# FoX layer of a two-layer trunk: V split as v^T and transposed by DMA, a query pair's scores and output products each in one block, and the opening's order written by hand

## The chip, the cores and the metric

The kernel runs on one core of a Trainium2 chip. The metric is the device time of one launch in microseconds (us), taken as the median of three runs.

## What is computed

`reference(x, ...)` runs two layers and a final norm on x of 1024 tokens by 1024 features, float32:

```python
for i in range(2):
    h = rmsnorm(x, norm_g[i])
    x = x + (fox_mixer(h, ...) if i == 0 else nsa_mixer(h, ...))
return rmsnorm(x, final_g)

def fox_mixer(h, w_in, b_f, w_out):            # 16 heads of 64
    q, k, v, f, z = split(h @ w_in)
    c = cumsum(log_sigmoid(f + b_f))            # one number per token and head
    logits = q @ k.T / 8 + c[query] - c[key]    # causal
    return (softmax(logits) @ v * silu(z)) @ w_out
```

The change concerns layer 0 (`fox_mixer`) alone. Layer 1, a sparse attention with three branches, follows layer 0's output projection.

## The kernel before

**Projections.** `to_hT` transposes the normed x on TensorE (PE) into `hT`, two halves of 512 tokens, each as a high and a low part (`fp32r`). A projection of 128 columns is `project` (L135): per half 8 steps of three 128x512 matmuls (`mm3`, L131 to L133: high by high, high by low, low by high), 24 in all. The weights of one head pair and kind are loaded by `load_w` (into the single buffer `wst`), split on VectorE and GpSimd, and kept two ahead in the queue `wq` by `next_w`.

**Head pairs.** The 16 heads go as 8 pairs p. `fox_fill` is the list of projections: for each pair K, V, Q and Z, with the forget gate behind pair 0's K. It may run up to two pairs ahead of the attention; it waits for `("scored", p - 2)` before K's buffers are written again and for `("done", p - 2)` before V's are.

**V.** `fox_v` copies the projection v^T (128 columns of a pair x 512 tokens) from PSUM to `vT` (ScalarE, L385), transposes it in four 128x128 blocks on PE into the PSUM tile `ptv` (L363, `fox_v_transposes`, issued four steps into the next projection), and splits it into three bf16 parts of 64 columns that stand side by side for each head and key tile: ScalarE (L366, L368), VectorE (L367), GpSimd (L369). So the 192 columns of a head's V are one run in `v`.

**Attention.** A `FoxDuo` is two query tiles of one head: u = 0 is tile 4 + x (5 to 8 key tiles), u = 1 is tile 3 - x; together 9 key tiles. `score(u)` makes the scores in pieces of up to 512 keys (two matmuls each, L523 and L524, into one of three PSUM buffers of `psS`), adds the bias and takes the running minimum on VectorE (L532), then takes the exponential (ScalarE, L541), a float16 high part (ScalarE, L542) and the low part (VectorE, L543) into `hl`, and sends both to `pT` by a transposing DMA (L544, on SP's queue). `pv(u)` multiplies with V: for each key tile a product of the high part with all 192 columns (L555) and one of the low part with 128 (L556), so a pair of products per key tile and 9 pairs per duo. `finish` sums the three parts on VectorE (L570), scales into `o` (L572), and after a pair's last duo transposes `o` on PE (L579, `pto`), multiplies with silu(z) and stores to `oF`.

**What sets the order.** `fox_main` runs 64 duos; step n does score(0) of duo n, pv(0) of duo n - 2, score(1) of duo n, pv(1) of duo n - 2, then `finish` of duo n - 2. Every generator yields a booked cost, and `merge` (L190) interleaves: after each yield of `fox_main` it runs `fox_fill` until the fill's booked sum has reached `PACE` (2.25, or `LAST` = 1.6 for the last eight duos) times what `fox_main` has booked. Booked are 650 per projection step, 450 per group of transposes, 570 per four pairs of products. `pv` yields after every four key tiles, so projections can come between. Engines run their instructions in this order; SP's DMA queue too.

**The opening.** A loop over the eight tiles of x loads, norms and transposes, two tiles behind; the norm's multiplies of tiles 2 and 5 are on GpSimd, the others on VectorE (L104). At tile 3, `next_w(False)` loads the first two weights, so `wst_v` stands on SP's queue ahead of the last tile, x_7. Then come K of pair 0, the forget gate, V of pair 0.

**The end.** When pair 7's projections are done, `load_wout` loads and splits the output weights in `hT`'s place, `out_start` starts the first tile of the output projection, and `out_layer` does the rest. `out_start` waits only for its last piece on `("o", 7, 1)`.

Of the kernel before, what the change touches and what calls it, by code (L numbers as in the profile page):

```python
# [33 lines left out]
def f(ap):  # L34
    return ap.bitcast(F32)
# [3 lines left out]
def tile_fox_nsa(ctx, tc, a, out):  # L39
# [212 lines left out]
    fox_order = [x for p in range(8) for x in ((1, p), (2, p), (0, p), (3, p))]  # L252
# [7 lines left out]
    gB = st.tile([P, D], F32, name="gB")  # L260
    pend = []
    for t in range(NT):
        xt = st.tile([P, D], F32, tag="x", bufs=7, name=f"x_{t}")
        dma(xt, a["x"][t * P:(t + 1) * P, :])
        if t == 0:
            dma(gB, a["norm_g"][0:1, :].to_broadcast([P, D]))
        nm = Norm(st, xt, f"n0_{t}", 3)
        nm.square(slice(0, D))
# [6 lines left out]
    for x in pend:  # L275
        to_hT(*x)
    dma(tri, a["tri"])


    wfst = st.tile([P, KC, H], F32, name="wfst")  # L280
    dma(wfst, a["fox_w_f"].rearrange("(k p) c -> p k c", p=P))
    bf = st.tile([H, 1], F32, name="bf")
    dma(bf, a["fox_b_f"].rearrange("o h -> h o"))
    below = st.tile([P, P], F32, name="below")
    dma(below, a["below"])
    wf = st.tile([P, KC, P], F32R, name="wf")
    G.tensor_copy(wf, zero[:, :, None].to_broadcast([P, KC, P]))
    V.tensor_copy(wf[:, :, 0:H], wfst)
    V.tensor_tensor(wf[:, :, 32:32 + H], wfst, f(wf[:, :, 0:H]), OP.subtract)

    def forget_gate():
        fT = st.tile([H, S], F32, name="fT")
        f2 = st.tile([H, S], F32, name="f2")
        for half in range(2):
            pt = ps_a(f"pf_{half}")
            ts = slice(half * 512, half * 512 + 512)
            for k in range(KC):
                T.matmul(pt, wf[:, k, :], hT[half][0][:, k, :], start=(k == 0), stop=False)
# [25 lines left out]
        V.tensor_tensor(e3[:, 1:, :], e3[:, 1:, :], r[:, 0:3, None].to_broadcast([P, 3, 32]), OP.add)  # L324
        pt = ps_t("pc")
# [8 lines left out]
    def fox_k(p):  # L334
        KH = [sa.tile([P, S], F32R, tag="KH", bufs=4, name=f"KH_{p}_{j}") for j in range(2)]
        KL = [sa.tile([P, S], F32R, tag="KL", bufs=4, name=f"KL_{p}_{j}") for j in range(2)]
        w = next_w()
        for half in range(2):
            ts = slice(half * 512, half * 512 + 512)
            pt = ps_a(f"k{p}_{half}")  # L340
            yield from project(w, hT, half, pt)
            for j in range(2):
                r, o = rows[j], rows[1 - j]
                A.copy(KH[j][r, ts], pt[r, :])
                V.tensor_tensor(KL[j][r, ts], pt[r, :], f(KH[j][r, ts]), OP.subtract)
                dma(f(KH[j][o, ts]), f(KH[j][r, ts]))
                dma(f(KL[j][o, ts]), f(KL[j][r, ts]))
        ready["k", p] = KH, KL

# [9 lines left out]
    def fox_v_transposes(vt, half, vT, name):  # L359

        pv = ps_t(f"ptv_{name}")
        for i in range(4):
            T.transpose(pv[:, i * P:(i + 1) * P], vT[:, i * P:(i + 1) * P], ident)  # L363
        v4, r = (x.rearrange("p (t j d) -> p j t d", t=4, j=2) for x in (pv, vT))
        v1, v2, v3 = (vt[:, :, 4 * half:4 * half + 4, 64 * i:64 * i + 64] for i in range(3))
        A.copy(v1, v4)  # L366
        V.tensor_tensor(r, v4, v1, OP.subtract)  # L367
        A.copy(v2, r)  # L368
        G.tensor_tensor(v3, r, v2, OP.subtract)  # L369

    def fox_v(p):
        w = next_w()
        vt = sa.tile([P, 2, NT, 192], BF16, tag="v", bufs=2, name=f"v_{p}")
        pend = []
        for half in range(2):
            pt = ps_a(f"v{p}_{half}")
            n = 0
            for c in project(w, hT, half, pt):
                yield c
                n += 1  # L380
                if n == 4 and pend:
                    fox_v_transposes(*pend.pop())
                    yield 450
            vT = sb[0].tile([P, 512], F32, tag="P", bufs=7, name=f"vT_{p}_{half}")
            A.copy(vT, pt)  # L385
            pend.append((vt, half, vT, f"{p}_{half}"))
        ready["v", p] = vt
        ready["later"] = pend

    def fox_q(p, w, halves=(1, 0)):  # L390
        Q = ready.setdefault(("qt", p), {})
        for half in halves:
            pt = ps_a(f"q{p}_{half}")
            n = 0
            for c in project(w, hT, half, pt):
                yield c
                n += 1
                if n == 4 and ready["later"]:
                    fox_v_transposes(*ready["later"].pop())
                    yield 450  # L400
# [16 lines left out]
    def fox_fill():  # L417
        for p in range(8):
            if p >= 2:
                yield lambda p=p: ("scored", p - 2) in ready  # L420
            yield from fox_k(p)
            if p == 0:
                yield from forget_gate()
                sb.append(tc.alloc_tile_pool(name="sb", bufs=2, reuse_waits="tile"))
            if p >= 2:
                yield lambda p=p: ("done", p - 2) in ready
            yield from fox_v(p)
            wo_copy(0, p)
# [8 lines left out]
    def out_start():  # L437
# [3 lines left out]
        for c in (slice(0, 4), slice(4, 7), slice(7, 8)):  # L441
            if c.stop == KC:
                yield lambda: ("o", 7, 1) in ready
# [38 lines left out]
    class FoxDuo:  # L482
# [19 lines left out]
        def score(self, u):  # L502
            p, j = self.p, self.j
            if u == 0:
                yield from self.pre()
# [10 lines left out]
            for c in range(s + 1):  # L516
# [4 lines left out]
                Ls.append((L, n))  # L521
# [17 lines left out]
            for c, (L, n) in enumerate(Ls):  # L539
# [6 lines left out]
        def pv(self, u):  # L546
# [38 lines left out]

    def fox_main():
        duos = [FoxDuo(p, j, x) for p in range(8) for j in range(2) for x in range(4)]
        for n in range(len(duos) + 2):
            if n == len(duos) - 8:
                yield (LAST,)  # L590
            for u in range(2):
                if n < len(duos):
                    yield from duos[n].score(u)
                    if u and duos[n].j == 1 and duos[n].x == 3:
                        ready["scored", duos[n].p] = True
# [732 lines left out]
```

## Time and profile before

| what | value |
| --- | --- |
| median of 3 runs | 1609.14 us (1608.29 to 1612.16) |
| the profiled execution's own time | 1609.73 us |
| its span in the profile | 1607.7 us |
| PE (matmul) busy | 1527.3 us, 95% |
| VectorE (DVE) busy | 1132.1 us, 70% |
| ScalarE (ACT) busy | 870.4 us, 54% |
| GpSimd (POOL) busy | 545.1 us, 34% |
| DMA, mean | 130 GB/s |

Layer 0 takes up to the last `finish` at 610.4 us and the output projection behind it. The page's shares are means over both layers. A line's busy time counts an instruction from its start to its modelled end; since matmuls are pipelined, the next one starts earlier than that, and what a matmul costs is read from one start to the next.

### The profile page before, as it was taken

To read this page: it belongs to the slowest core of one execution; us is meant where nothing else is said; L and a number is where in the kernel's file an instruction comes from. 1 tells how busy PE (TensorE), PEld (TensorE's weight loads), DVE (VectorE), ACT (ScalarE), POOL (GpSimd) and SP (SyncE) were. 2 spreads that over 40 slices of the span, in tenths; PEclk is the share of its full clock that TensorE was granted. 3 is DMA by queue.
4 is the path that set the end of the run, shared out by engine and by line. 5 is a ranking of instruction groups with operands and counts; after the bars stand their busy time and mean duration, and the time that the engine had idled before them with its cause. 6 is when DMAs were issued, how large, how long until landed. Compare 5 with 4: busy or idle time off the path is not lost.

```text
span 1607.7 us, 26181 instructions
## 1 busy us (share of the span) xinstructions
PE 1527.3 (95%) x8600; PEld 1269.1 (79%) x8600; DVE 1132.1 (70%) x2867; ACT 870.4 (54%) x2126; POOL 545.1 (34%) x584
## 2 busy tenths in 40 slices
PE   6999999999999868999999989999999999999898
PEld 5887777777777656878888777788888888888786
DVE  6377777777777884355654686788888888888633
ACT  5255545555555662223232545578778778787522
POOL 3232223323223110032333223446646547554200
PEclk9999999999999979999999999999999999999999
DMA  7676666657657675441535645511312312212442
GB/s 241 226 143 134 128 160 131 153 113 149 156 114 160 151 153 165 133 155 60 162 104 154 218 151 193 204 54 63 122 53 66 119 40 79 73 40 93 147 148 92
DMA packets 237431, 209.11 MB, mean 130 GB/s; under 512 B 162737, under 2 KB 184497, under 8 KB 237041
## 3 DMA queue, kind: packets, MB, share of 16 engines
q1 hardware_dynamic: 237296, 207.46, 47.3%
q8 instruction: 68, 1.11, 0.3%
q14 instruction: 67, 0.54, 0.1%
HBM read 123.26 MB, written 46.20 MB: 105 GB/s over the span
## 4 chain that ended last, share of the span: by engine, by line
PE 60%; DVE 18%; ACT 9%; issue 7%; DMA 4%; POOL 1%; SPq 0%; DVEq 0%; POOLq 0%; ACTq 0%
PE ptp_n L1186 6%; PE S_n L1162 6%; DVE P L532 4%; PE y L131 3%; PE y L132 3%; PE y L133 3%; PE O_n L1195 3%; PE O_n L1194 3%; DVE hl L543 3%; ACT P L541 3%; DMA wo<-wD 1%; ACT cP L969 1%; PE nz L131 1%; ACT hl L542 1%; PE nz L132 1%
## 5 line engine op out<-in xcount | busy, mean ns | idle before, releaser
L1174 POOL TENSOR_SCALAR P_n<-P_n,l_n,gates 128x640 f32<-128x640 f32 (+7 forms) x256 | 200.9, 791 | 179.8 <-DVE l_n L1172 146.0
L541 ACT ACTIVATE P<-P,m 128x256 f32<-128x256 f32 (+1 forms) x192 | 117.0, 610 | 164.2 <-DVE m L532 163.8
L144 DVE TENSOR_TENSOR ptl_n<-ptp_n,pth_n 128x512 fp32r<-128x512 f32 (+1 forms) x272 | 181.4, 672 | 33.8 <-ACT pth_n L143 30.1
L1170 ACT ACTIVATE P_n<-P_n,m_n 128x640 f32<-128x640 f32 (+7 forms) x256 | 188.5, 737 | 24.9 <-DVE m_n L1169 22.8
L143 ACT CAST pth_n<-ptp_n 128x512 fp32r<-128x512 f32 (+1 forms) x272 | 153.8, 569 | 72.7 <-PE ptp_n L1186 71.5
L1186 PE MATMUL ptp_n<-ident,P_n 128*128 128x128 f32 x1056 | 167.1, 275 | 5.4 <-DVE ptl_n L144 3.6
L1162 PE MATMUL S_n<-nk,nq 128*128 128x320 f32 (+5 forms) x768 | 171.1, 333 | 0.2 <-DVE m_n L1169 0.2
L512 POOL TENSOR_TENSOR Bd<-B,tri 128x128 f32<-128x128 f32 x128 | 65.0, 509 | 302.3 <-DVE m L532 284.9
L1186 PEld LDWEIGHTS ptp_n<-ident,P_n 128*128 128x128 f32 x1056 | 124.4, 140 | 31.9 <-DVE ptl_n L144 9.3
L1194 PE MATMUL O_n<-pth_n,nv 128*128 128x512 f32 (+3 forms) x384 | 140.1, 369 | 1.0 <-DVE ot_n L1205 0.7
L543 DVE SCALAR_TENSOR_TENSOR hl<-P,hl 128x256 f16<-128x256 f32 (+1 forms) x192 | 126.4, 686 | 19.4 <-ACT hl L542 17.8
L1162 PEld LDWEIGHTS S_n<-nk,nq 128*128 128x128 f32 x768 | 128.0, 188 | 15.2 <-DVE m_n L1169 1.6
L1195 PE MATMUL O_n<-ptl_n,nv 128*128 128x512 f32 (+3 forms) x384 | 120.6, 338 | 0.1
L1169 DVE CUSTOM_DVE_ANT_0 P_n<-S_n,wmask 128x128 f32<-128x128 f32 (+1 forms) x192 | 113.3, 591 | 9.0 <-PE S_n L1162 4.1
L555 PE MATMUL O<-v,pT 128*128 128x192 bf16 x576 | 104.1, 255 | 12.3 <-DMA pT<-hl 10.8
L131 PE MATMUL y<-wo,oh 128*128 128x512 f32 x256 | 103.1, 403 | 9.0 <-ACT oh L627 4.0
L132 PE MATMUL y<-wo,oh 128*128 128x512 f32 x256 | 102.3, 400 | 0.0
L133 PE MATMUL y<-wo,ol 128*128 128x512 f32 x256 | 101.4, 397 | 0.0
L555 PEld LDWEIGHTS <-pT 128*128 128x128 f16 x576 | 57.4, 100 | 54.6 <-issue 40.4
L556 PE MATMUL O<-v,pT 128*128 128x128 bf16 x576 | 97.7, 224 | 0.0
L542 ACT ACTIVATE hl<-P 128x256 f16<-128x256 f32 (+1 forms) x192 | 92.5, 513 | 2.5 <-DMA pT<-hl 0.8
L1194 PEld LDWEIGHTS O_n<-pth_n,nv 128*128 128x128 f32 x384 | 72.6, 189 | 7.0 <-DVE ot_n L1205 1.3
(346 smaller groups left out, 4077.7 us busy)
## 6 DMA issues: line engine op xcount, KB each, us to landing
nq<-qD SPq DMA_DIRECT2D x64, 256.0 KB
B<-cD SPq DMA_DIRECT2D x16, 512.0 KB
wo<-wD SPq DMA_DIRECT2D x16, 512.0 KB
nq<-qD SPq DMA_DIRECT2D x64, 128.0 KB
of<-oF SPq DMA_DIRECT2D x14, 512.0 KB
x<-in_x_dram SPq DMA_DIRECT2D x8, 512.0 KB
wst_k<-in_fox_w_dram SPq DMA_DIRECT2D x8, 512.0 KB
wst_v<-in_fox_w_dram SPq DMA_DIRECT2D x8, 512.0 KB
```

What stands on the lines that cost most here:

```text
L131: T.matmul(ps, wh, mh, start=first, stop=False, **kw)
L132: T.matmul(ps, wh, ml, start=False, stop=False, **kw)
L144: V.tensor_tensor(lo[:, 0:n], pt[:, 0:n], f(hi[:, 0:n]), OP.subtract)
L541: A.activation(L[:, 0:n], L[:, 0:n], AF.Exp, bias=init, scale=-1.0, accum_out=self.lr[:, col + c:col + c + 1])
L543: V.scalar_tensor_tensor(lo[:, cs], L[:, 0:n], UP, hi[:, cs], OP.mult, OP.subtract)
L555: T.matmul(po[:, 0:192], self.hT[:, b0 + k, :], v[:, self.j, k, :], start=(k == 0), stop=False)
L1162: T.matmul(ps[:, b, 0:w], self.q[x][:, qi * P:(qi + 1) * P], k[:, k0 + b * w:k0 + b * w + w], start=(x == 0), stop=(x == 1))
L1170: A.activation(L, L, AF.Exp, bias=m, scale=-1.0, accum_out=lr[:, 0, qi:qi + 1])
L1174: G.tensor_scalar(L, L, lr[:, 1, qi:qi + 1], gates[:, i, x:x + 1], OP.mult, OP.mult)
L1186: T.transpose(pt[:, (x + i) * P:(x + i + 1) * P], L[:, kb * P - k0:(kb + 1) * P - k0], ident)
L1194: T.matmul(po[:, d], v, hi[:, c], start=(b == i == 0), stop=False)
L1195: T.matmul(po[:, d], v, lo[:, c], start=False, stop=(b == len(self.blocks) - 1 and i == len(pieces) - 1))
```

## The change

**V.** `fox_v` splits v^T itself, straight from PSUM, into three bf16 rows of 512 in `vs` (one buffer): ScalarE (L397, L399), VectorE (L398), GpSimd (L400). One transposing DMA per half (L401, 12 blocks of 128x128) puts them in `v`. There is no group of transposes on PE, no `vT` and no `ptv`. In `v` the three parts of a key tile now lie 512 elements apart, so that a product's right operand is three runs of 64.

**Blocks.** Step n of `fox_main` does the scores of both tiles of duo n (the short one first, and within a tile the last piece first), and then all nine pairs of products of duo n - 2 followed by `finish`; `burst` sums the booked costs and yields once, so that no projection comes between.

**Opening.** A function orders PE, VectorE and ScalarE by hand: all eight norms on VectorE, each tile transposed one step behind its norm, only K's weights loaded by it, x_7 before `wst_v` on SP's queue, and the forget gate's and K's steps mixed in from tile 5 on. K of pair 0 is a generator `k0`, the gate `gate0`.

**End.** `out_start` waits for each of its pieces by its own `("o", p, 1)`.

```diff
-    def fox_v_transposes(vt, half, vT, name):
...
     def fox_v(p):
         w = next_w()
-        vt = sa.tile([P, 2, NT, 192], BF16, tag="v", bufs=2, name=f"v_{p}")
...
+        v = sa.tile([P, 2, 3, 4, P], BF16, tag="v", bufs=2, name=f"v_{p}")
         for half in range(2):
             pt = ps_a(f"v{p}_{half}")
...
+            yield from project(w, hT, half, pt)
+            vs = sa.tile([P, 3, 512], BF16, tag="vs", bufs=1, name=f"vs_{p}_{half}")
...
+            A.copy(vs[:, 0], pt)
+            V.tensor_tensor(r, pt, vs[:, 0], OP.subtract)
+            A.copy(vs[:, 1], r)
+            G.tensor_tensor(vs[:, 2], r, vs[:, 1], OP.subtract)
+            nc.sync.dma_start_transpose(v[:, half].rearrange("p c t d -> p (c t) d"), vs.rearrange("p c t -> p (c t)"))
...
     def fox_q(p, w, halves=(1, 0)):
...
-                if n == 4 and ready["later"]:
-                    fox_v_transposes(*ready["later"].pop())
-                    yield 450
+            yield from project(w, hT, half, pt)
...
-            for c in range(s + 1):
+            for c in range(s, -1, -1):
...
+            po = po[:, 0:192].rearrange("p (c d) -> p c d", c=3)
             for k in range(nk):
-                T.matmul(po[:, 0:192], self.hT[:, b0 + k, :], v[:, self.j, k, :], start=(k == 0), stop=False)
-                T.matmul(po[:, 0:128], self.hT[:, b0 + nk + k, :], v[:, self.j, k, 0:128], start=False, stop=(k == nk - 1))
-                if k % 4 == 3:
-                    yield 570
-            if nk % 4:
-                yield 142 * (nk % 4)
+                vk = v[:, k // 4, :, k % 4, 64 * self.j:64 * self.j + 64]
+                T.matmul(po, self.hT[:, b0 + k, :], vk, start=(k == 0), stop=False)
+                T.matmul(po[:, 0:2], self.hT[:, b0 + nk + k, :], vk[:, 0:2], start=False, stop=(k == nk - 1))
+            yield 142 * nk
...
-            for u in range(2):
-                if n < len(duos):
-                    yield from duos[n].score(u)
...
-                if n >= 2:
-                    yield from duos[n - 2].pv(u)
+            if n < len(duos):
+                yield from burst(duos[n].score(u) for u in (1, 0))
...
             if n >= 2:
+                yield from burst(duos[n - 2].pv(u) for u in (0, 1))
                 yield from duos[n - 2].finish()
```

and of the opening:

```diff
-        h = nm.finish(gB, 1, G if t in (2, 5) else None)
-        pend.append((h, t, hT, f"n0_{t}", (ps_s, ps_t)))
-        if t >= 2:
-            to_hT(*pend.pop(0))
-        if t == 3:
-            next_w(False)
...
+        with tc.manual_schedule(engines={T.engine, V.engine, A.engine}):
+            for t in range(NT + 1):
+                if t < NT:
+                    nm = Norm(st, xs[t], f"n0_{t}", 3)
+                    nm.square(slice(0, D))
+                    hs[t] = nm.finish(gB)
+                if t:
+                    to_hT(hs.pop(t - 1), t - 1, hT, f"n0_{t - 1}", (ps_s, ps_t))
+                if t == 1:
+                    V.tensor_copy(whi, wst)
+                    G.tensor_tensor(wlo, wst, f(whi), OP.subtract)
...
+                if t == 4:
...
+                    side = [k0] * 9 + [gate0] * 8
+                if t >= 5:
+                    for g in side[0:5]:
+                        next(g)
...
```

In PE's order up to the output projection there are 174 blocks of output products before and 66 now; behind 144 and 52 of them stands a projection matmul. Layer 1's order is unchanged.

PE at the end of pair 1 (k3 is the K projection of pair 3, O_1_1_3 the products of the pair's last duo, pto its o transposes), before:

```order
L131 MATMUL k3_1_2326<-hT0_1_0_96,whi_k3_2046 128x512
L132 MATMUL k3_1_2326<-hT0_1_1_97,whi_k3_2046 128x512
L133 MATMUL k3_1_2326<-hT0_1_0_96,wlo_k3_2047 128x512
L555 LDWEIGHTS pT_1_1_3_2063
L555 MATMUL O_1_1_3_2280<-v_1_868,pT_1_1_3_2063 128x192
L556 LDWEIGHTS pT_1_1_3_2063
L556 MATMUL O_1_1_3_2280<-v_1_868,pT_1_1_3_2063 128x128
L131 MATMUL k3_1_2326<-hT0_1_0_96,whi_k3_2046 128x512
L132 MATMUL k3_1_2326<-hT0_1_1_97,whi_k3_2046 128x512
L133 MATMUL k3_1_2326<-hT0_1_0_96,wlo_k3_2047 128x512
L579 MATMUL pto_1_1_2344<-ident_72,o_1_1668 128x128 x3
```

And now, the last pair of products, then the projection matmuls up to the transposes (of twelve, six are left out):

```order
L567 LDWEIGHTS pT_1_1_3_2046
L567 MATMUL O_1_1_3_2282<-v_1_861,pT_1_1_3_2046 128x192
L568 LDWEIGHTS pT_1_1_3_2046
L568 MATMUL O_1_1_3_2282<-v_1_861,pT_1_1_3_2046 128x128
L131 MATMUL k3_1_2309<-hT0_1_0_96,whi_k3_2023 128x512
L132 MATMUL k3_1_2309<-hT0_1_1_97,whi_k3_2023 128x512
L133 MATMUL k3_1_2309<-hT0_1_0_96,wlo_k3_2024 128x512
...
L132 MATMUL k3_1_2309<-hT0_1_1_97,whi_k3_2023 128x512
L133 MATMUL k3_1_2309<-hT0_1_0_96,wlo_k3_2024 128x512
L588 MATMUL pto_1_1_2327<-ident_72,o_1_1656 128x128 x4
L131 MATMUL k3_1_2309<-hT0_1_0_96,whi_k3_2023 128x512
```

The products are no longer split by projections; between the last of them and the transposes stand twelve projection matmuls instead of three.

ScalarE at the V projection of pair 2 (P and hl rows are the exponentials and high parts of the scores), before:

```order
L385 COPY vT_2_0_1726<-v2_0_1646 128x512
L541 ACTIVATE P_1_0_3_1_0_1736,l_1_0_3_1676<-P_1_0_3_1_0_1736,m_1_0_3_1_1734 128x128
L542 ACTIVATE hl_1_0_3_1674<-P_1_0_3_1_0_1736 128x128
L366 CAST v_2_1645<-ptv_2_0_1777 128x2x4x64
L541 ACTIVATE P_1_1_0_0_0_1770,l_1_1_0_1765<-P_1_1_0_0_0_1770,m_1_1_0_0_1768 128x512
L368 CAST v_2_1645<-vT_2_0_1726 128x2x4x64
L542 ACTIVATE hl_1_1_0_1763<-P_1_1_0_0_0_1770 128x512
L541 ACTIVATE P_1_1_0_0_1_1787,l_1_1_0_1765<-P_1_1_0_0_1_1787,m_1_1_0_0_1768 128x128
L542 ACTIVATE hl_1_1_0_1763<-P_1_1_0_0_1_1787 128x128
L385 COPY vT_2_1_1834<-v2_1_1728 128x512
L541 ACTIVATE P_1_1_0_1_0_1829,l_1_1_0_1765<-P_1_1_0_1_0_1829,m_1_1_0_1_1827 128x512
```

And now (vs is the split's buffer, of which there is one; the row vs_2_1 is the first to write it for the second half):

```order
L397 CAST vs_2_0_1729<-v2_0_1643 128x512
L399 CAST vs_2_0_1729<-vr_2_0_1730 128x512
L551 ACTIVATE P_1_1_0_1_0_1766,l_1_1_0_1761<-P_1_1_0_1_0_1766,m_1_1_0_1_1764 128x512
L551 ACTIVATE P_1_1_0_0_1_1779,l_1_1_0_1761<-P_1_1_0_0_1_1779,m_1_1_0_0_1777 128x128
L552 ACTIVATE hl_1_1_0_1759<-P_1_1_0_1_0_1766 128x512
L552 ACTIVATE hl_1_1_0_1759<-P_1_1_0_0_1_1779 128x128
L551 ACTIVATE P_1_1_0_0_0_1784,l_1_1_0_1761<-P_1_1_0_0_0_1784,m_1_1_0_0_1777 128x512
L397 CAST vs_2_1_1823<-v2_1_1736 128x512
L552 ACTIVATE hl_1_1_0_1759<-P_1_1_0_0_0_1784 128x512
L399 CAST vs_2_1_1823<-vr_2_1_1824 128x512
```

The copy to `vT` and the casts out of `ptv` have gone; the second half's first copy now stands with five score instructions between it and the first half's second one. Counted so, there are 0 in pair 0, 6, 5, 5, 6 and 6 in pairs 1 to 5, 1 in pair 6 and 6 in pair 7.

PE at the end of the projections (z7_0 is the last one), before:

```order
L556 LDWEIGHTS pT_6_1_2_5938
L556 MATMUL O_6_1_2_6139<-v_6_4757,pT_6_1_2_5938 128x128
L523 MATMUL S_7_0_1_0_0_6194<-KH_7_0_5340,Q_7_1_0_5830 128x512
L524 MATMUL S_7_0_1_0_0_6194<-KL_7_0_5342,Q_7_1_0_5830 128x512
L131 MATMUL z7_0_6099<-hT0_0_0_94,whi_z7_5720 128x512
L132 MATMUL z7_0_6099<-hT0_0_1_95,whi_z7_5720 128x512
L133 MATMUL z7_0_6099<-hT0_0_0_94,wlo_z7_5721 128x512
L523 MATMUL S_7_0_1_0_1_6202<-KH_7_0_5340,Q_7_1_0_5830 128x256
L524 MATMUL S_7_0_1_0_1_6202<-KL_7_0_5342,Q_7_1_0_5830 128x256
L579 MATMUL pto_6_1_6273<-ident_72,o_6_5640 128x128 x2
L555 LDWEIGHTS pT_6_1_3_6033
```

And now:

```order
L568 LDWEIGHTS pT_6_1_1_5820
L568 MATMUL O_6_1_1_6036<-v_6_4703,pT_6_1_1_5820 128x128
L131 MATMUL z7_0_5976<-hT0_0_0_94,whi_z7_5615 128x512
L132 MATMUL z7_0_5976<-hT0_0_1_95,whi_z7_5615 128x512
L133 MATMUL z7_0_5976<-hT0_0_0_94,wlo_z7_5616 128x512
L131 MATMUL z7_0_5976<-hT0_0_0_94,whi_z7_5615 128x512
L132 MATMUL z7_0_5976<-hT0_0_1_95,whi_z7_5615 128x512
L133 MATMUL z7_0_5976<-hT0_0_0_94,wlo_z7_5616 128x512
L533 MATMUL S_7_0_0_1_0_6087<-KH_7_0_5267,Q_7_0_0_5798 128x512
L534 MATMUL S_7_0_0_1_0_6087<-KL_7_0_5269,Q_7_0_0_5798 128x512
L588 MATMUL pto_6_1_6222<-ident_72,o_6_5626 128x128
L567 LDWEIGHTS pT_6_1_2_5909
```

The last projection matmul stood among the scores of duo S_7_0_1 and behind products of O_6_1_2; now it stands before the first score of duo S_7_0_0 and behind O_6_1_1.

## Rows read from the trace of the kernel before

**Rows 1.** The page: the span, and each engine's busy time in us, its share of the span and its number of instructions.

```profile
span 1607.7 us, 26181 instructions
...
PE 1527.3 (95%) x8600; PEld 1269.1 (79%) x8600; DVE 1132.1 (70%) x2867; ACT 870.4 (54%) x2126; POOL 545.1 (34%) x584
```

**Rows 2.** The table by stretches: start and end in us and length; busy time in us (and instructions) of PE, its weight loads, VectorE, ScalarE and GpSimd; then PE's granted clock as a share, the DMA engines' busy share, and GB/s.

```profile
80.00:547.00 467.00, 458.61 (x2740) 363.87 (x2738) 355.45 (x1002) 246.25 (x608) 138.42 (x151) 1.00 0.65 138
...
556.00:600.00 44.00, 27.04 (x172) 21.08 (x173) 38.53 (x126) 28.97 (x78) 5.68 (x11) 0.73 0.78 159
```

**Rows 3.** VectorE in order of time: five of the 64 reductions of output products, one per duo: the first, the 54th, the 56th, the 59th and the last. Start in us, busy us, engine, line, operation, output and inputs, sizes; in brackets the idle time before and what ended it.

```profile
100.19 0.55 DVE L570 TENSOR_REDUCE ot<-O 128x128 f32<-128x384 f32 x1
...
546.91 0.54 DVE L570 TENSOR_REDUCE ot<-O 128x128 f32<-128x384 f32 x1
...
572.22 0.54 DVE L570 TENSOR_REDUCE ot<-O 128x128 f32<-128x384 f32 x1
...
589.13 0.56 DVE L570 TENSOR_REDUCE ot<-O 128x128 f32<-128x384 f32 x1
...
610.42 0.56 DVE L570 TENSOR_REDUCE ot<-O 128x128 f32<-128x384 f32 x1 [3.66 <-PE O L556]
```

**Rows 4.** PE in order of time, 302.35 to 303.8 us, columns as in rows 3. A block of output products between two V projection matmuls.

```profile
302.35 0.39 PE L133 MATMUL v<-hT,wlo_v 128*128 128x512 f32 x1
302.58 0.26 PE L555 MATMUL O<-v,pT 128*128 128x192 bf16 x1
302.67 0.22 PE L556 MATMUL O<-v,pT 128*128 128x128 bf16 x1
302.73 0.25 PE L555 MATMUL O<-v,pT 128*128 128x192 bf16 x1
...
303.09 0.22 PE L556 MATMUL O<-v,pT 128*128 128x128 bf16 x1
303.12 0.47 PE L131 MATMUL v<-hT,whi_v 128*128 128x512 f32 x1
303.43 0.39 PE L132 MATMUL v<-hT,whi_v 128*128 128x512 f32 x1
```

**Rows 5.** The same view at 521.7 us: a group of four transposes of V between products and a Q projection.

```profile
521.73 0.22 PE L556 MATMUL O<-v,pT 128*128 128x128 bf16 x1
521.78 0.61 PE L363 MATMUL ptv<-ident,vT 128*128 128x128 f32 x4
522.15 0.47 PE L131 MATMUL q<-hT,whi_q 128*128 128x512 f32 x1
```

**Rows 6.** Groups of PE's instructions from 80 to 547 us: line, output and inputs, count | busy us, mean ns of one | idle us before them and what ended most of it.

```profile
L555 PE MATMUL O<-v,pT 128*128 128x192 bf16 x486 | 86.1, 249 | 1.6 <-DVE ot L570 1.2
...
L363 PE MATMUL ptv<-ident,vT 128*128 128x128 f32 x56 | 8.6, 275 | 0.6 <-ACT vT L385 0.6
...
L579 PE MATMUL pto<-ident,o 128*128 128x128 f32 x48 | 7.9, 280 | 5.5 <-DVE o L572 5.5
```

**Rows 7.** The instructions that touch `vT`: count, shortest/median/longest in ns, first and last start, forms.

```profile
L385 ACT COPY vT<-v x16: 562/587/589, 53.6 to 518.0; 128x512 f32<-128x512 f32 x16
...
L369 POOL TENSOR_TENSOR v<-vT,v x16: 1161/1168/1592, 64.0 to 528.5; 128x512 bf16<-128x512 f32 x16
```

**Rows 8.** The DMA view of 100 to 500 us: packets, and the queue's packets, MB and the share of 16 engines.

```profile
DMA packets 121795, 55.98 MB, mean 140 GB/s; under 512 B 112799, under 2 KB 112799, under 8 KB 121759
...
q1 hardware_dynamic: 121759, 55.53, 65.5%
```

**Rows 9.** The issues of the scores' transposing DMAs on SP's queue, columns as in rows 7.

```profile
L544 SPq DMA_TRANSPOSE pT<-hl x128: 1168/1442/3741, 87.8 to 606.2; - x128
```

**Rows 10.** PE in order of time at 560 us, where the granted clock is 1.2 GHz.

```profile
560.22 0.37 PE L555 MATMUL O<-v,pT 128*128 128x192 bf16 x1
560.38 0.31 PE L556 MATMUL O<-v,pT 128*128 128x128 bf16 x1
560.49 0.37 PE L555 MATMUL O<-v,pT 128*128 128x192 bf16 x1
```

**Rows 11.** The chain of waits between 575 and 612 us: start, us, and the step; here the landing of such a transpose.

```profile
604.30 4.28 DMA pT<-hl
```

**Rows 12.** PE in order of time, four matmuls of the opening: the first, two that follow one another, and the first of V.

```profile
21.27 0.50 PE L131 MATMUL k<-hT,whi_k 128*128 128x512 f32 x1 [1.71 <-ACT hT L118]
...
24.04 0.63 PE L132 MATMUL k<-hT,whi_k 128*128 128x512 f32 x1
24.47 0.63 PE L133 MATMUL k<-hT,wlo_k 128*128 128x512 f32 x1
...
46.97 0.39 PE L131 MATMUL v<-hT,whi_v 128*128 128x512 f32 x1
```

**Rows 13.** VectorE in order of time from 6 to 17 us: the norms' reciprocals and multiplies, hT's low parts, and the cast of K's weights.

```profile
6.96 1.28 DVE L104 SCALAR_TENSOR_TENSOR h_n<-x,st_n,gB 128x1024 f32<-128x1024 f32 x1 [0.54 <-DMA gB<-in_norm_g_dram]
...
10.08 0.69 DVE L119 TENSOR_TENSOR hT<-pth_n,hT 128x512 fp32r<-128x512 f32 x1 [1.83 <-ACT hT L118]
...
12.07 0.15 DVE L100 RECIPROCAL st_n<-st_n 128x1 f32<-128x1 f32 x1
...
12.74 1.26 DVE L126 CAST whi_k<-wst_k 128x1024 fp32r<-128x1024 f32 x1
...
14.85 2.43 DVE L104 SCALAR_TENSOR_TENSOR h_n<-x,st_n,gB 128x1024 f32<-128x1024 f32 x1
```

More of the change, by code (lines that the diff above doesn't have):

```diff
@@ L250, in wsec @@
         return load_w(wp, a["fox_w"][kind * 8 + p], f"{'qkvz'[kind]}{p}")
-    fox_order = [x for p in range(8) for x in ((1, p), (2, p), (0, p), (3, p))]
+    fox_order = [x for p in range(8) for x in ((1, p), (2, p), (0, p), (3, p))][1:]
     wq = []
@@ L357, in v_transposes @@
         V.tensor_tensor(vt[:, :, 4 * half:4 * half + 4, 64:128], v4, f(hi), OP.subtract)
-    def fox_v_transposes(vt, half, vT, name):
[L361 to L369, printed above, removed]
     def fox_v(p):
         w = next_w()
-        vt = sa.tile([P, 2, NT, 192], BF16, tag="v", bufs=2, name=f"v_{p}")
-        pend = []
+        v = sa.tile([P, 2, 3, 4, P], BF16, tag="v", bufs=2, name=f"v_{p}")
         for half in range(2):
             pt = ps_a(f"v{p}_{half}")
[L377 to L382, printed above, removed]
-                    yield 450
[L384 to L388, printed above, removed]
+            yield from project(w, hT, half, pt)
+            vs = sa.tile([P, 3, 512], BF16, tag="vs", bufs=1, name=f"vs_{p}_{half}")
+            if p:
+                r = sb[0].tile([P, 512], F32, tag="P", bufs=7, name=f"vr_{p}_{half}")
+            else:
+                r = f(sa.tile([P, 512], F32R, tag="Q", bufs=8, name=f"vr_{p}_{half}"))
+            A.copy(vs[:, 0], pt)
[3 more added lines that the diff above has]
+            nc.sync.dma_start_transpose(v[:, half].rearrange("p c t d -> p (c t) d"), vs.rearrange("p c t -> p (c t)"))
+        ready["v", p] = v
     def fox_q(p, w, halves=(1, 0)):
@@ L393, in fox_q @@
             pt = ps_a(f"q{p}_{half}")
[L394 to L397, printed above, removed]
-                if n == 4 and ready["later"]:
-                    fox_v_transposes(*ready["later"].pop())
-                    yield 450
+            yield from project(w, hT, half, pt)
             for j in range(2):
@@ L420, in fox_fill @@
                 yield lambda p=p: ("scored", p - 2) in ready
-            yield from fox_k(p)
+            yield from k0 if p == 0 else fox_k(p)
             if p == 0:
-                yield from forget_gate()
-                sb.append(tc.alloc_tile_pool(name="sb", bufs=2, reuse_waits="tile"))
+                for _ in range(11):
+                    yield next(gate0)
             if p >= 2:
@@ L427, in fox_fill @@
             yield from fox_v(p)
+            if p == 0:
+                yield from gate0
+                sb.append(tc.alloc_tile_pool(name="sb", bufs=2, reuse_waits="tile"))
             wo_copy(0, p)
@@ L503, in score @@
             p, j = self.p, self.j
-            if u == 0:
+            if u == 1:
                 yield from self.pre()
@@ L538, in score @@
             col = 0 if u else 1
-            for c, (L, n) in enumerate(Ls):
+            for c, L, n in Ls:
                 cs = slice(512 * c, 512 * c + n)
@@ L584, in finish, with burst @@
                     yield 450
+    def burst(gens):
+        cost = 0.0
+        for g in gens:
+            for c in g:
+                if callable(c):
+                    yield c
+                else:
+                    cost += c
+        yield cost
     def fox_main():
@@ L590, in fox_main @@
                 yield (LAST,)
-            for u in range(2):
-                if n < len(duos):
-                    yield from duos[n].score(u)
-                    if u and duos[n].j == 1 and duos[n].x == 3:
-                        ready["scored", duos[n].p] = True
-                if n >= 2:
-                    yield from duos[n - 2].pv(u)
+            if n < len(duos):
+                yield from burst(duos[n].score(u) for u in (1, 0))
+                if duos[n].j == 1 and duos[n].x == 3:
+                    ready["scored", duos[n].p] = True
             if n >= 2:
+                yield from burst(duos[n - 2].pv(u) for u in (0, 1))
                 yield from duos[n - 2].finish()
```

55 lines of the change are left out of this document (34 added, 21 removed).

## The prediction, made before the changed kernel was run

> **What bounds the kernel now.** I read the page first: TensorE (PE) is busy 95% of a span of 1607.7 us, VectorE 70% [rows 1]. Such a mean mixes stages, so next the table by stretches [rows 2]: from 80 to 547 us, layer 0's long middle, PE is busy 458.6 of 467 us at a granted clock of 1.00, VectorE 355.5, ScalarE 246.3, the DMA engines 65%; from 556 to 600 us PE is busy 27 of 44 us at a clock of 0.73 and VectorE 38.5. So layer 0 has a part in which every nanosecond taken off PE's queue is a nanosecond of time, and an end in which PE waits for others. The diff touches nothing of layer 1, and the end of layer 0 is the only door to it: the sum is made up to the last reduction of output products, at 610.4 us [rows 3].
>
> Third view, PE in order of time [rows 4]. The busy column overlaps (0.39 us for a matmul after which the next starts 0.23 later), so I take start-to-start times. A projection matmul: 0.23. A pair of output products (192 and 128 columns): 0.14. Behind a block of output products the first projection matmul holds PE 0.31 instead of 0.23, and the last product before it 0.03 instead of 0.06: each return from output products to projections costs 0.05 to 0.08 us, whatever the block's length.
>
> **The change, part by part.**
>
> *V without TensorE.* Eight head pairs x two halves x four = 64 transposes leave PE. One group holds it from 521.78 to 522.15, 0.37 us, with 0.03 of changing over [rows 5]: 16 x 0.40 = **-6.4 us**, all of it in the part where PE is full, bar 0.6 us of idling before them [rows 6]. With it goes a 0.59 us copy per half on ScalarE [rows 7], which bounds nothing there: 0. VectorE and GpSimd still do one subtraction a half each. Added are 16 DMA transposes of 12 blocks; a pair's scores need 144 such blocks, so at most a sixth is added to a share of 65.5% of the DMA engines [rows 8]: 0 to 11 points, up to 76%. V is read a whole pair later, so its landing is covered; SP's queue takes 1.4 us more for each issue [rows 9], twice in some 67 us. Cost 0.
>
> *Blocks of output products.* In the instruction order of both programs there are 174 blocks before, 66 now, of which 144 and 52 are followed by projections. 92 returns fewer x 0.06 = **-5.5 us** (4.6 to 7.4). The score matmuls gain nothing by standing together: no return after them shows in the rows.
>
> *The o transposes at a pair's end.* They wait for VectorE's last reduction: PE stood 5.5 us in four such waits [rows 6]. Before, at most three projection matmuls lie between the last product and the first transposes; now 9 to 15, that is 2.1 to 3.5 us of cover. I take **-3 us** (0 to -5.5).
>
> *The reading of V.* The new right operand is three runs of 64 elements, where every matmul of the trace reads one run. Unknown. Below: no change, 0.14 a pair, the nearest row, since columns and type are the same [rows 4]. Above: the same products at the lower clock, 0.27 a pair [rows 10]. A gain is excluded: no column is saved. I take 0, as 128 bytes in a row is far from element by element. Against this edit speaks the Trainium skill, "Advanced Engine Details and Errata", section PSUM Cachelines, by which any non-contiguous access pattern significantly slows down matmuls; no run here shows it. By it the sum would be that of rival 2 instead of this one.
>
> *The end of layer 0.* The fill's cost per pair falls by the 900 that the transposes were booked with, but the pace (2.25) stays, so projections run out earlier: behind S_6_1_3 instead of S_7_0_1's large tile. That moves 1.7 duos of scores and one of output products out of the full part: 9 x 0.14 + 1.7 x 1.05 (1152 columns twice, at the rate of 512 in 0.23) = -3.0 us there. They come back in the end, where the reductions go at 4.3 us a duo over the last five steps (589.1 to 610.4), against 8.4 before (100.2 to 546.9 in 53) and 12.7 in the two steps where the casts of the output weights and their loads cut in [rows 3]. 1 to 1.7 duos x 4.3 = 4.3 to 7.3, taken as +6. Together **+3 us** (+1.3 to +18 if they fall among the 12.7 steps).
>
> *ScalarE behind the one buffer vs.* Half 1's first copy must wait until half 0's transpose has read vs: GpSimd 1.17, issue 1.44, landing 4.28 [rows 7, 9, 11] = 6.9 us after half 0's second copy. The exponentials queue behind it. In the order five or six score instructions, a duo's share of some 8 us, lie between in six pairs, one in pair 6, none in pair 0 where no scores wait yet. And the products had room: among the causes of PE's 1.6 us of idling before them in the middle, the transposes of the scores don't stand [rows 6]. **+1 us** (0 to 4).
>
> *The opening.* Before, the first projection matmul starts at 21.27, they go at 0.43 us each (1.2 GHz) at first, with transposes and gaps between, and forget gate and K are done at 46.97 [rows 12]. Now VectorE does all eight norms. Up to tile 3 in hT it has five multiplies of 1.28, four reciprocals of 0.15, eight subtractions of 0.69 and a cast of 1.26: 13.8 us from 6.96, plus the 1.83 for which it waits behind tile 0, plus 1.15 for a multiply beside GpSimd's split of K's weights (2.43 instead of 1.28) [rows 13]: first matmul at about 23.7. It starts 2.4 us later, but five tiles are transposed by then and no gap follows, and tile 7 no longer waits behind wst_v on SP's queue. **0** (-1.5 to +1.5).
>
> Sum: -6.4 - 5.5 - 3 + 3 + 1 = -10.9 us on the profiled execution's 1609.73. The median of the runs is 0.6 lower, so 1609.1 - 10.9 = **1598 us**.
>
> **Rivals.**
>
> 1. *Given back in the end.* If the duos that lose their projections fall among the 12.7 us steps, 1.7 x 12.7 = 21.6 us stand against 3 + 14.9 saved. With +1: 1613.8, no change within what can be told. For it: the output weights' casts stay in the same queues. Against: their loads start when the projections end, earlier now, and the end is only one duo longer.
>
> 2. *Slower: the strided V.* Place: the 576 pairs of products. Price by the rows: up to 0.13 each, 75 us, so up to 1673. It decides from 0.02 a pair (10.9 / 576): above 0.16 instead of 0.14 the gain is gone. Against: each run is as long as half the old row.
>
> 3. *ScalarE's wait reaches PE.* If each of eight pairs waited 6.9 us and half of it came through, +27.6 less the 1 booked: 1625. From 1.4 us a pair on the gain is gone. Against: the room above.
>
> 4. *The bursts fall apart.* The order shows them whole up to the end of the projections; in the end four are cut. Then -6.4 and -3 alone remain with the +4: about 1604, the edge of no change.
>
> 5. *More.* If the larger ends hold (-6.4, -7.4, -5.5, +1.3, 0, -1.5): 1590; if the two 12.7 steps shorten too, 1586.
>
> **How the numbers follow.** 0.3% is 4.8 us, about what can be told from no change. The forecast with its own range (1592 to 1604): 0.62. Rival 1: 0.14. Rival 2: 0.04. Rival 3: 0.06. Rival 4: 0.04. Rival 5: 0.10. Faster by over 4.8 us: 0.60 of the forecast, all of rival 5, 0.02 of rival 1 and 0.02 of rival 4, 0.74. Slower: rivals 2 and 3 but for 0.02 that stays small, and 0.01 of rival 1, 0.09. The rest, 0.17, is the same. The range: from rival 5's 1586 up to 1609, which takes in rivals 4 and 5 and half of rival 1; the rest of rival 1 (0.07), rivals 2 and 3 but for 0.02 (0.08) lie above it, and some 0.04 below.
>
> **What would show it.** Right: no transposes of V on PE; products at 0.14 a pair in runs of 18; duos at 8.1 us in the middle, not 8.4; waits for o under 2.5 us; the last projection near 537 us and the last reduction near 599.5, with layer 1 as long as before (997 us). Wrong: pairs above 0.16 (rival 2); waits of the products for pT before the projections end, with ScalarE idle at vs (rival 3); reductions at over 10 us in more than two steps (rival 1); VectorE or DMA ending waits in the opening, with V's first matmul after 49 us.

## The result, and the profile after

The changed kernel takes 1591.77 us (1591.07 to 1594.45), the kernel before 1609.14 in the same five rounds: ratio 0.9897, 95% interval 0.9882 to 0.9913. That is 17.4 us where 10.9 were forecast; the time lies in the range, nearer to its low end of 1586 than to the forecast of 1598. Every time below is the median of a kernel's undisturbed executions; two of V alone at the pace 2.2, of 1687.63 and 2989.87 us, ran in a slower state and are left out.

The page after, against [rows 1]:

```profile
span 1589.7 us, 26075 instructions
...
PE 1510.2 (95%) x8536; PEld 1270.7 (80%) x8536; DVE 1135.9 (71%) x2869; ACT 862.3 (54%) x2110; POOL 531.5 (33%) x580
```

64 matmuls fewer are the transposes of V. PE's busy share is the same, so where the 18 us of span went needs places in the program. Three instructions cut layer 0: the first V matmul, the last projection matmul (of z7), the last reduction. In order of time after, PE twice and then VectorE:

```profile
48.35 0.40 PE L131 MATMUL v<-hT,whi_v 128*128 128x512 f32 x1
...
532.14 0.39 PE L133 MATMUL z<-hT,wlo_z 128*128 128x512 f32 x1
...
594.39 0.56 DVE L579 TENSOR_REDUCE ot<-O 128x128 f32<-128x384 f32 x1 [4.03 <-PE O L568]
```

The same of the kernel before: V at 46.97 [rows 12], the reduction at 610.42 [rows 3], and between them

```profile
555.13 0.40 PE L133 MATMUL z<-hT,wlo_z 128*128 128x512 f32 x1
```

| stretch | before | after | difference | forecast |
| --- | --- | --- | --- | --- |
| opening, to V's first matmul | 47.0 | 48.4 | +1.4 | 0 |
| full part, to the last projection | 508.2 | 483.8 | -24.4 | -16.9 |
| end, to the last reduction | 55.3 | 62.3 | +7.0 | +6 |
| rest (layer 1's order is the same) | 997.3 | 995.3 | -2.0 | 0 |

The rest varies from 993.9 to 998.4 over the traces of this study, all with the same code there: its 2 us are not the change's. So the end came as forecast, and the full part brought 7.5 us more.

In the full part, PE from 80 to 530 us (columns as in [rows 2]), before and then after:

```profile
80.00:530.00 450.00, 442.72 (x2636) 351.45 (x2635) 341.75 (x958) 236.56 (x585) 136.50 (x147) 1.00 0.66 139
```

```profile
80.00:530.00 450.00, 445.55 (x2687) 371.03 (x2686) 352.78 (x992) 236.65 (x589) 133.11 (x150) 1.00 0.73 157
```

PE stood 7.3 us before and 4.4 after; the DMA engines are at 0.73, where up to 0.76 was forecast. What PE still waits for, from 48 to 533 us (us in total, times, longest), to be held against [rows 6]:

```profile
PE pto L588 <- DVE o L581: 3.9, 3, 1.8
PE S L533 <- DVE m L542: 0.5, 1, 0.5
```

A return from products to projections, after; PE, and then its weight loads:

```profile
160.71 0.25 PE L567 MATMUL O<-v,pT 128*128 128x192 bf16 x1
160.79 0.22 PE L568 MATMUL O<-v,pT 128*128 128x128 bf16 x1
160.85 0.25 PE L567 MATMUL O<-v,pT 128*128 128x192 bf16 x1
160.93 0.22 PE L568 MATMUL O<-v,pT 128*128 128x128 bf16 x1
160.96 0.47 PE L131 MATMUL v<-hT,whi_v 128*128 128x512 f32 x1
161.27 0.39 PE L132 MATMUL v<-hT,whi_v 128*128 128x512 f32 x1
161.50 0.40 PE L133 MATMUL v<-hT,wlo_v 128*128 128x512 f32 x1
```

```profile
160.85 0.10 PEld L568 LDWEIGHTS <-pT 128*128 128x128 f16 x1
160.93 0.19 PEld L131 LDWEIGHTS v<-hT,whi_v 128*128 128x128 f32 x1
161.04 0.19 PEld L132 LDWEIGHTS v<-hT,whi_v 128*128 128x128 f32 x1
```

Two readings. A pair of products takes 0.14 us (160.71 to 160.85) as in [rows 4], although V is read in three runs. And a return still costs 0.31 for the first projection matmul (160.96 to 161.27). The load of its weights takes 0.19 us, where a product's takes 0.10, and starts with the last product, 0.03 before the matmul itself; that this is why the return costs more is argued, not shown.

### The profile page after: what moved, and what is told of

It is laid out like the page before. It is cut to its first block, busy times and chain, and to the rows that moved or that the text cites. A ratio compares the mean times of both kernels' runs of the same rounds, so it can differ in the third digit from the quotient of the medians.

```text
span 1589.7 us, 26075 instructions
## 1 busy us (share of the span) xinstructions
PE 1510.2 (95%) x8536; PEld 1270.7 (80%) x8536; DVE 1135.9 (71%) x2869; ACT 862.3 (54%) x2110; POOL 531.5 (33%) x580
## 4 chain that ended last, share of the span: by engine, by line
PE 77%; DVE 10%; ACT 6%; DMA 4%; issue 3%; POOL 1%; SPq 0%; DVEq 0%; ACTq 0%; POOLq 0%
PE ptp_n L1204 7%; PE S_n L1180 6%; PE y L131 3%; PE y L132 3%; PE O_n L1213 3%; PE y L133 3%; PE O_n L1212 3%; PE O L567 3%; PE q L131 2%; PE S L534 2%; PE S L533 2%; PE q L133 2%; PE q L132 2%; PE v L131 2%; PE v L133 2%
## 5 line engine op out<-in xcount | busy, mean ns | idle before, releaser
L551 ACT ACTIVATE P<-P,m 128x512 f32<-128x512 f32 (+1 forms) x192 | 116.9, 609 | 135.5 <-DVE m L542 134.5
L522 POOL TENSOR_TENSOR Bd<-B,tri 128x128 f32<-128x128 f32 x128 | 59.8, 482 | 234.5 <-DVE m L542 228.3
L553 DVE SCALAR_TENSOR_TENSOR hl<-P,hl 128x512 f16<-128x512 f32 (+1 forms) x192 | 122.4, 652 | 21.1 <-ACT hl L552 19.7
L567 PE MATMUL O<-v,pT 128*128 128x192 bf16 x576 | 92.2, 254 | 9.6 <-DMA pT<-hl 9.5
L552 ACT ACTIVATE hl<-P 128x512 f16<-128x512 f32 (+1 forms) x192 | 92.4, 513 | 4.7 <-DMA pT<-hl 3.2
L568 PE MATMUL O<-v,pT 128*128 128x128 bf16 x576 | 89.6, 225 | 0.0
```

Source lines behind the costliest of these rows:

```text
L567: T.matmul(po, self.hT[:, b0 + k, :], vk, start=(k == 0), stop=False)
```

## The experiments

All ratios are to the kernel before, run on the same chip, with 95% intervals. "Duos" are those whose scores / products stand before the last projection matmul in PE's order; the two spans are read from each trace as above (0.3% is 4.8 us). A trace is of one execution: those of both blocks alone at 2.25 and of the products' blocks alone are the shortest of their five, 4.9 and 4.4 us under the medians. Some 3 us of that lie in the rest behind layer 0, at its shortest there (993.9 and 994.1); a part may lie in their spans.

| kernel | ratio | pace | duos | full part | end |
| --- | --- | --- | --- | --- | --- |
| before | 1 | 2.25 | 57.3 / 55 | 508.2 | 55.3 |
| changed | 0.9897 (0.9882 to 0.9913) | 2.25 | 56 / 54 | 483.8 | 62.3 |
| V alone | 0.9995 (0.9981 to 1.0008) | 2.25 | 55.7 / 53.4 | 503.8 | 61.2 |
| V alone | 0.9964 (0.9951 to 0.9976) | 2.2 | 57.7 / 55 | 503.6 | 54.7 |
| both blocks alone | 0.9886 (0.9866 to 0.9906) | 2.25 | 58 / 55 | 489.3 | 55.1 |
| both blocks alone | 0.9925 (0.9913 to 0.9937) | 2.3 | 56 / 54 | 486.7 | 63.4 |
| products' blocks alone | 0.9885 (0.9869 to 0.9901) | 2.25 | 57.3 / 55 | 489.7 | 55.2 |
| changed | 0.9856 (0.9842 to 0.9869) | 2.2 | 58 / 55 | 484.0 | 54.9 |
| changed | 0.9849 (0.9835 to 0.9864) | 2.15 | 59 / 57 | 491.4 | 43.5 |
| changed | 0.9850 (0.9828 to 0.9873) | 2.1 | 60.3 / 58 | 497.0 | 37.8 |

### The parts by themselves

V alone: the kernel before with the new `fox_v`, and products that read its layout.

```diff
-                    fox_v_transposes(*pend.pop())
+            nc.sync.dma_start_transpose(v[:, half].rearrange("p c t d -> p (c t) d"), vs.rearrange("p c t -> p (c t)"))
```

> The kernel before with V's new split and DMA transposes alone: the order of scores and products stays interleaved, the opening is the old one; of the end, each piece of the output stage waits for its own pair. Theory 1 (the terms as the two traces give them): the transposes' 6.3 us, 1.0 of waiting before them and 0.6 of returns behind them go from PE's full part, about -8; in the order the projections end 1.6 duos earlier, which gives back about 3 in the end: about 1604 us, and products still 0.14 us a pair although V is read in three runs. Theory 2 (V is most of the change's gain, because it also frees ScalarE and PSUM): 1597 or less. Theory 3 (the end doesn't give back): 1601.

Measured 1608.54 us: no difference. The end gave back 5.9 us, and the full part is only 4.4 shorter, of which the 1.6 duos that left it are over 3: there PE waits anew for products behind VectorE's work on V and Q. PE's waits from 48 to 533 us in this kernel:

```profile
PE pto L559 <- DVE o L552: 6.4, 3, 3.5
PE O L535 <- DVE vr L369: 2.9, 2, 2.4
PE O L535 <- DVE Q L384: 1.6, 2, 1.1
PE O L535 <- DVE ot L550: 0.7, 1, 0.7
```

Theory 1 had the give-back, but too small, and not these waits.

The blocks alone: `score`, `pv`, `burst` and `fox_main` of the change, V as before.

```diff
+                yield from burst(duos[n].score(u) for u in (1, 0))
...
+                yield from burst(duos[n - 2].pv(u) for u in (0, 1))
```

> The kernel before with the scores and the products of a duo each in one block, the transposes of V on PE and the old opening kept. Theory 1: 91 fewer returns from products (5.3), the entries into blocks (3), the returns from scores (2.2) and the waits for o (2.2) go, and in the order the projections end where they did: about 1596.5 us. Theory 2 (what the prediction booked for blocks and waits, 5.5 and 3, and nothing for the scores): 1600.6.

Measured 1590.88, as fast as the whole change. Both sizes were too small. PE is busy all but 0.2 us of the stretch that had 7.3 of idling, and the one wait left from 48 to 533 us is 0.2:

```profile
80.00:530.00 450.00, 449.83 (x2748) 376.11 (x2746) 357.69 (x1008) 245.35 (x609) 135.53 (x153) 1.00 0.66 143
```

```profile
PE ptv L363 <- ACT vT L385: 0.2, 1, 0.2
```

Only the products in a block, the scores as before between projections:

```diff
-                yield from burst(duos[n].score(u) for u in (1, 0))
+                for u in (1, 0):
+                    yield from duos[n].score(u)
```

> The kernel before with the products of a duo in one block, but projections still between its score pieces (in the new order of pieces); V's transposes on PE, old opening. Theory 1 (the returns from products are the larger half of the blocks' 18.9 us): returns and entries 7 us, and the returns from scores stay: 1600 to 1602, with PE's 7 us of waits in the middle still there. Theory 2 (the products in one block also end the waits for o and for pT): about 1593 to 1595. Theory 3 (the scores in one block end them): over 1602.

Measured 1590.99: theory 2, and further than it said. No gain is left for the scores' standing together: 0.9885 without it and 0.9886 with it, though the intervals would leave room for some 4 us. This kernel keeps the new order of the scores (the short tile first, the last piece first, both tiles ahead of the products); what that order does by itself was not run. The full part holds exactly the work of before (57.3 / 55), so its 18.5 us can be split by start-to-start times: the projections behind products 7.8 less, the last products of blocks 1.6 more (together the returns, 6.2); the waits for o 6.4, of which the waits view names 5.5; entries into products, scores and V's transposes 3.9; the rest 2.

The 3.9 is no price of an entry. The median entry from a projection into products takes 0.238 us before and 0.230 here, a plain projection step 0.23. Nine long entries before stand 4.5 us above that, two here 1.5. Of the nine, the waits view of before, from 48 to 556 us, names

```profile
PE O L555 <- DVE ot L570: 1.2, 3, 0.6
PE S L523 <- DVE l L568: 0.8, 1, 0.8
PE ptv L363 <- ACT vT L385: 0.6, 1, 0.6
```

So of the 18.5 us a third is the returns and about half waits for other engines: 6.4 for o and some 3 at entries.

### The pace

Beside V itself, the projections' early end is what V alone and the changed kernel share. Three kernels differ from others by one number:

```diff
-    PACE, LAST = 2.25, 1.6
+    PACE, LAST = 2.2, 1.6
```

The changed kernel at 2.2:

> The changed kernel with the pace 2.2 instead of 2.25: in the order the projections end at duo 58 of the scores and 55 of the products, as with the blocks alone, instead of 56 and 54. Theory 1 (the projections' early end gives V's gain back): the end, 62 us from the last projection to the last reduction, is 55 again, the full part is 3.4 longer: about 1588 us. Theory 2 (V's gain is lost in waits on PE in the middle): 1591 to 1592, and waits for o as now.

Measured 1585.40. Theory 1, and 6 instead of 3.5: the end is 54.9, and the full part took the added work (2 duos of scores, one of products) without growing, for the most part since the waits for o fell from 3.9 to 1.3. The two instructions that bound its end:

```profile
532.21 0.39 PE L133 MATMUL z<-hT,wlo_z 128*128 128x512 f32 x1
```

```profile
587.07 0.56 DVE L579 TENSOR_REDUCE ot<-O 128x128 f32<-128x384 f32 x1 [5.76 <-PE O L568]
```

The mirror, the blocks alone at 2.3:

> The blocks alone (no DMA transposes of V, old opening) at the pace 2.3, at which the projections end at duo 56 of the scores and 54 of the products, where they end in the changed kernel, instead of 58 and 55; each piece of the output stage waits for its own pair. Theory 1 (the pace and not V decides): the end is 62 us long instead of 55, the full part 3.4 shorter, and waits for o come back: 1594 to 1597 us. Theory 2 (the end given back is V's own doing): 1591.

This kernel takes over the change's waits of the output stage: without them, at this pace, that stage would read a piece of `oF` before it is written. Measured 1595.50, theory 1; without any edit of V the end grows by 8.3. Of the waits for o only 1.0 came back, against 3.9 in the changed kernel and 3.2 in the changed kernel with the old opening, all with the same work in the full part: most of those came with V. The instructions that bound the end:

```profile
532.16 0.40 PE L133 MATMUL z<-hT,wlo_z 128*128 128x512 f32 x1
```

```profile
595.52 0.56 DVE L566 TENSOR_REDUCE ot<-O 128x128 f32<-128x384 f32 x1 [4.86 <-PE O L555]
```

V alone at 2.2:

> V's split and DMA transposes alone, as in the run of V alone, at the pace 2.2: the projections end at duo 57.7 of the scores and 55 of the products, as in the kernel before (57.3 and 55). Theory 1 (V's 6 to 8 us of PE were all given back in the end): 1601 to 1603 us. Theory 2 (without the blocks the waits of the products on VectorE, 5 us, and for o, 6, which came with V, take it too): 1606 to 1608.

Measured 1602.5, theory 1, and apart from V alone at 2.25 (1608.54), although the waits for o are there (5.9). So V is worth some 5 to 6 us once the projections end where they did: 5.8 without the blocks (1 to 0.9964), 4.8 with them (0.9886 to 0.9856). The second number is the looser: those two intervals overlap, and that step also brings the new opening and the change's waits of the output stage.

Lower still, the changed kernel at 2.15:

> The changed kernel at the pace 2.15: the projections end at duo 59 of the scores and 57 of the products. Theory 1 (each duo moved out of the end goes at PE's rate instead of 4.3 us): one duo of scores and two of products more in the full part, 3.6 us, and up to 6 less in the end than at 2.2: 1582 to 1584. Theory 2 (the end's length is set by the output weights, whose loads start when the projections end): 1585 to 1589.

and at 2.1:

> The changed kernel at the pace 2.1: the projections end at duo 60 of the scores and 58 of the products. Theory 1: 1580 to 1583. Theory 2 (the end is set by the output weights): 1587 or more; and with less projection work to a duo, VectorE makes PE wait in the middle.

Measured 1583.12 and 1581.63, theory 1's numbers, but with both terms larger: the end shrinks by 11.4 and 17.1 from 54.9, the full part grows by 7.4 and 13.0, where 6 and 3.6 were expected at 2.15. The end's length follows the pace, so theory 2 is out. Against 2.2 neither time can be told apart by its interval. At 2.1, 2.5 us of waits for Q stand in the full part, on VectorE, as theory 2 had it; its price did not come. By their medians these are the fastest kernels of the study, 1.5% below the kernel before.

### ScalarE's wait for the one buffer

After, in pair 2, SP's queue and then ScalarE:

```profile
172.25 4.33 SPq L554 DMA_TRANSPOSE pT<-hl  x1
176.67 1.46 SPq L401 DMA_TRANSPOSE v<-vs  x1
```

```profile
177.04 0.19 ACT L551 ACTIVATION_READ_ACCUMULATOR P<-P,m 128x1 f32 x1
180.57 0.59 ACT L397 CAST vs<-v 128x512 bf16<-128x512 f32 x1 [3.34 <-DMA v<-vs]
```

ScalarE stands 14.5 us so, in four waits. Three are of this kind; the longest, in pair 0, has no transpose of scores ahead of it, only the issue and landing of V's own:

```profile
58.03 1.40 SPq L401 DMA_TRANSPOSE v<-vs  x1
```

```profile
63.11 0.59 ACT L397 CAST vs<-v 128x512 bf16<-128x512 f32 x1 [6.35 <-DMA v<-vs]
```

I tried to shorten the wait where GpSimd's part is:

```diff
-            G.tensor_tensor(vs[:, 2], r, vs[:, 1], OP.subtract)
+            V.tensor_tensor(vs[:, 2], r, vs[:, 1], OP.subtract)
```

> The changed kernel with the split's last subtraction (the third part of V) on VectorE instead of GpSimd. Theory 1 (in GpSimd's queue it stands behind additions that wait for the scores' minima, so V's transpose lands late, ScalarE stands 14.5 us at the one buffer, and the waits for o, 3.9 us on PE, are its echo): ScalarE's wait at vs under 7 us, PE's waits for o under 2, about 1588 us. Theory 2 (the wait is the issue and landing of the transpose itself, and VectorE, given 16 x 0.68 = 11 us more, delays o): unchanged or slower, 1591 to 1594.

Measured 1592.38 (0.9898, 0.9885 to 0.9912): unchanged; ScalarE's wait is 15.2, the waits for o 3.6. Theory 1 has fallen. The rows above show what it overlooked: three times V's transpose stands behind one of the scores on SP's queue, whose issue took 4.33 in the case shown, and in pair 0 ScalarE goes on only 3.68 after the issue's end.

With the pace 2.2 as well:

> The two edits together, VectorE for the third part and the pace 2.2. If both first theories hold, 1584 to 1585 us, 6 below the blocks alone, which is what the transposes of V take on PE; if only the end gives back, 1588; if neither, 1591 to 1593.

Measured 1585.18 (0.9848, 0.9834 to 0.9861), what the pace alone gives: "only the end gives back", with a larger size than written. With the pace 2.2 alone ScalarE even waits 18.7 us at vs, and PE's waits are 1.6 in all: little of it can reach PE there. A second buffer was not tried; as the kernel's buffers stand, SBUF has no room for it.

### The opening

The kernel before with the new opening, and the changed kernel with the old one:

```diff
-        h = nm.finish(gB, 1, G if t in (2, 5) else None)
...
+                    hs[t] = nm.finish(gB)
```

> The kernel before with the new opening alone. Theory 1 (V's first matmul at 48.35 instead of 46.97 us in the traces): 1.4 us slower, about 1610.5. Theory 2 (what the opening loses on PE it wins in the first scores, since V of pair 0 no longer waits): 1607 to 1608.

> The changed kernel with the old opening. Theory 1: V's first matmul 1.4 us earlier, about 1590.4 us. Theory 2 (the new opening pays later): 1593 or more.

Measured 1610.00 (1.0015, 1.0003 to 1.0026) and 1593.45 (0.9910, 0.9894 to 0.9926), theory 1 and theory 2: alone it costs some 2 us, within the change no cost can be told from nothing. Over the traces V's first matmul comes at 45.4 to 47.5 us with the old opening and 47.2 to 48.7 with the new; the trace of before was one of the late ones. With V, blocks and the old opening the first scores come too early for Q:

```profile
72.98 0.50 PE L501 MATMUL S<-KH,Q 128*128 128x512 f32 x1 [1.74 <-DVE Q L384]
```

The blocks alone, with the same opening, don't show that wait, and they have no buffer `vs`. In the changed kernel with the old opening, the trace shows where the wait comes from: ScalarE waits at vs for the transpose of pair 0's first half, and the second half's split then stands ahead of Q on ScalarE. ScalarE, and then VectorE, which writes the Q that the scores wait for:

```profile
69.75 0.59 ACT L368 CAST vs<-v 128x512 bf16<-128x512 f32 x1 [3.57 <-DMA v<-vs]
71.10 0.62 ACT L370 CAST vs<-vr 128x512 bf16<-128x512 f32 x1 [0.76 <-DVE vr L369]
71.62 0.58 ACT L383 ACTIVATE Q<-q 64x512 fp32r<-64x512 f32 x1
```

```profile
72.24 0.68 DVE L384 SCALAR_TENSOR_TENSOR Q<-q,Q 64x512 fp32r<-64x512 f32 x1 [0.58 <-ACT Q L383]
```

So here ScalarE's wait does reach PE, with 1.7 us. With the new opening the same wait ends at 63.11, and PE doesn't wait there.

## Why the prediction was right, and where it was not

- **Sign and range held**, over a range wide enough to touch no change, by a sum whose largest term was too small: 8.5 us were booked for the blocks of products with the waits for o, and the full part falls by 18.5 in the kernel that has the products' blocks and the new order of the scores alone. Of the 18 us between the two traces, the rest's 2.0 are luck.
- **Returns**: 5.5 (4.6 to 7.4) forecast, 6.2 measured. Count and price were right.
- **The o transposes**: 3 (0 to 5.5) forecast. With blocks alone it was 6.4, the whole wait and more, since the 0.9 us beyond the waits view counts as spacing. In the changed kernel 3.9 of the 5.5 remained, at 2.2 only 1.3; the sign "under 2.5" failed. I took the middle for no better reason than that it was the middle, and it was too little there and too much here. The step that failed is that the cover decides. In pair 1 twelve projection matmuls, 2.9 us, follow the last product, and PE waits all the same, because VectorE starts the reduction only 3.18 us after that product:

```profile
216.52 0.22 PE L568 MATMUL O<-v,pT 128*128 128x128 bf16 x1
...
221.70 0.33 PE L588 MATMUL pto<-ident,o 128*128 128x128 f32 x1 [1.81 <-DVE o L581]
```

```profile
219.70 0.55 DVE L579 TENSOR_REDUCE ot<-O 128x128 f32<-128x384 f32 x1
```

- **Not booked**: the waits at entries into products, scores and transposes, 3.9 net in the kernel with the products' blocks. The waits view of before has most of them, in small lines.
- **V**: 6.4 less 1 for the buffer forecast. At equal work the full part shows 5.3 (489.3 to 484.0, the blocks alone and the changed kernel at 2.2) and 2.9 (486.7 to 483.8, the blocks alone at 2.3 and the changed kernel). At the pace as it stands it brought nothing: blocks alone 0.9886, with V 0.9897.
- **The end**: +6 forecast, +7.0 measured; the mirror experiment shows that it is the pace's doing. Rival 1 had the right place and a price (21.6) that did not come.
- **Rival 2 is out**: 0.14 a pair as before. The Trainium skill, "Advanced Engine Details and Errata", section PSUM Cachelines, says that any non-contiguous access pattern significantly slows down matmuls. That section is about PSUM, and here PSUM is written in one run of 192; the three runs are of the right operand, in SBUF. For that operand, in runs of 128 bytes, the trace shows no slowing; for PSUM no run here tests the sentence.
- **Rival 3**: ScalarE does stand, 14.5 us in all. Its way to PE exists: 1.7 us of it arrive with the old opening. In the changed kernel none arrives at the first scores, and how much of the 3.9 us of waits for o comes from it is not shown; its price (27.6) did not come.
- **Rival 5** had a number nearer to the time (1590), but not by its terms: the o transposes' 5.5, the shorter end and the faster opening did not come.
- **The opening**: 0 (-1.5 to +1.5) forecast, +1.4 between the two traces, +2.4 us by the ratio of the opening alone. K's first matmul came at 23.82, as forecast (23.7); what failed is that the later start would be made up.
- **Other signs**: duos at 8.3 us (the first reduction at 95.3, the 54th at 535.9) where 8.1 was forecast, the last projection at 532.1 where 537 was, the last reduction at 594.4 where 599.5 was.

## What to carry to other kernels

Where one work fills another's gaps at a fixed pace, work taken out of the filler moves the filler's end: set the pace anew with the edit, or the gain stands in a table of terms and not in the time. Put short matmuls in one long block: each way out costs, 0.05 to 0.08 us here, and the projections that no longer split them become cover for the wait behind, which was worth more. Cover ends a wait only if the engine waited for is not late itself: look at when it starts, in the order after the edit, before pricing the term.

## What the runs showed of the hardware

- A right operand in three runs of 64 bf16 elements costs TensorE nothing: 0.14 us a pair.
- A projection's weight load takes 0.19 us, a product's 0.10; the first projection matmul behind a product holds PE 0.31 instead of 0.23.
- A transposing DMA's issue held SP's queue 4.33 us where 1.4 is usual [rows 9], and the next transpose with it.
